# Seven block products in place of eight for two projections of an mLSTM and attention layer

## The chip, the cores and the metric

The kernel runs on one core of one Trainium2 chip. The metric is the device time of one execution in microseconds (us); a kernel's time is the median of its runs. The engines are called PE (TensorE, the matrix products), DVE (VectorE), ACT (ScalarE), POOL (GpSimd) and SP (SyncE, whose queue issues the weight loads). Each runs its own instructions strictly in the order in which they stand, apart from PE's weight loads, and semaphores tie the engines together.

## The reference

One layer on 512 tokens of width 1024, with 16 learned meta tokens ahead of them. The input is normalised, `h = rms_norm(x)`, and one large product `z = h @ w_in` is cut into the inputs of two branches: a forgetting attention with 8 heads ("FoX") and an mLSTM with 4 heads. Cut to what matters here:

```python
z = h @ w_in
(fq, fk, fv, ff, fz, mqk, mv, mi, mf, mo, mz, ga, gb) = jnp.split(z, SPLIT_POINTS, axis=-1)
...
hb = mlstm_scan(mq, mk, mv, log_ib, log_fb)                 # 4 heads, value width 512 each
hb = jax.nn.sigmoid(mo).reshape(B, L, 4, 512) * hb          # the gate "mo", 2048 columns of w_in
hb = rms_norm(hb, g_head.reshape(4, 512)).reshape(B, L, 2048)
yb = (hb * jax.nn.silu(mz)) @ w_b                           # "mz", 2048 columns of w_in
merged = jax.nn.sigmoid(ga) * ya + jax.nn.sigmoid(gb) * yb
return x + rms_norm(merged @ w_o, g_post)
```

The two projections that the change touches are `mo` and `mz`: per head, 512 tokens by 1024 times 1024 by 512 each.

## The kernel before

**Products.** Every fp32 product is three products of a faster type: a matrix is split into a high part (ACT, Copy, L121) and a low part (DVE, matrix minus high part, L123), and `mm3` (L128 to L131) accumulates high by high, high by low and low by high in PSUM. `hh` and `hl` are the parts of the transposed, normalised input (8 slices of 128 rows, 528 tokens) and are made once. A weight chunk of 128 x 1024 fp32 is loaded by SP (`wload`, tag `raw`, 3 buffers), split by ACT and DVE (`wsplit`, tags `whi` and `wlo`, 4 buffers), and used by PE.

**PSUM.** `psum2` is a pool of two tiles of two banks, `psum1` one of four tiles of one bank. A product that wants a `psum2` tile waits until the readers of the tile two before are through.

**The mLSTM heads** (L626 to L651, four rounds): `decay(h)` (row `nm` from memory, POOL adds a mask to make `dm`, ACT makes 14 blocks of `w` by Exp), `turn_part(h-1)` (PE transposes `ht` to `pht`, times `gz`, split into `bh` and `bl`), `conv_part` for q and for k (products `pqk`, ACT to `z` and `y`, three DVE steps for the taps, sigmoid `sg`, split into `qkh`, `qkl`), `wb_part(h-1)` (products `pyb`), `v_part`, `score_part` (products `ps`, times `w`, split into `wh`, `wl`), `mo_part`, `value_part`, `mz_part`. A scheduler then fixes the order of each engine's instructions, and mixes neighbouring parts.

- `mo_part` (L534 to L541): 96 matmuls 128x512 into two `psum2` tiles `po`, tokens on the partitions, then a sigmoid of each tile (L540) to `so`.
- `value_part` (L558 to L593): for each of four token chunks c, 6(c+1)+2 matmuls (`pna`, `pnb` for c = 0 and 1 in `psum1` tiles, `pnc` for c = 2 and 3 in `psum2` tiles), `r` from the normaliser, `ht` = product times `r` times `so` (L583), the square sum (ACT, L587), its power on POOL (`mrs`, L590), and the scaling of `ht` (L591).
- `mz_part` (L543 to L556): for u = 0 and 1, 48 matmuls 128x512 into one `psum2` tile `pz`, channels on the partitions, a sigmoid (L551), and two DVE steps (L554) to `gz`.

After the heads come the FoX branch, the gates, `w_a`, `w_o` and the output norm, which the change touches only in where tiles lie.

## Time and profile before

| | |
|---|---|
| median of 3 runs | 978.28 us (978.22 to 979.26) |
| the profiled execution | 978.2 us, span 976.4 us from the first to the last instruction |
| mean granted PE clock | 0.993 |
| matmuls, all | 5211 |
| from one head's first transposes to the next head's | 131.3 us |
| PE waits, longest | 3.4 us at 13.67 us; 1.5 us at 61.9 us |

The profile lists instructions by line, engine, operation and tile, with the start and the length of each. The length of a matmul is modelled and overlaps the next one; what a matmul costs in a full stream is the step from one start to the next. What lies outside the span, 1.8 us, is taken as fixed.

### The profile page before, as it was taken

What the parts mean: (1) busy time and instruction counts of PE and PEld (TensorE: products, weight loads), DVE (VectorE), ACT (ScalarE), POOL (GpSimd) and SP (SyncE); (2) the same over time, 40 slices, a digit from 0 to 9 for tenths busy, and PEclk for the clock granted to TensorE, in tenths of its full rate; (3) what the DMA queues carried; (4) which work ended last, traced back from release to release, by engine and by line L of the source; (5) the groups of instructions that cost most, each with busy time, mean ns of one, the idle gap of its engine ahead of it and who ended that gap; (6) DMA issues with size and microseconds to landing.
All of it is one profiled execution on the core that took longest, in us unless ns stands there. A gap on an engine that the chain in (4) does not pass through costs nothing.

```text
span 976.4 us, 12876 instructions
## 1 busy us (share of the span) xinstructions
PE 960.7 (98%) x5211; PEld 821.2 (84%) x5211; DVE 478.2 (49%) x792; ACT 376.6 (39%) x575; POOL 100.7 (10%) x164
## 2 busy tenths in 40 slices
PE   7999999999999999999999999999999999999997
PEld 5998889888898888988888888898888888888887
DVE  4795457344385235662444454446235446333443
ACT  4547335144252253441322333336233355322231
POOL 2152101001000001010000010214111112100000
PEclk7999999999999999999999999999999999999999
DMA  6233122323213322233232332333232322522312
GB/s 202 87 93 104 56 87 87 109 65 97 65 65 109 86 80 65 73 107 87 65 93 87 115 114 66 93 115 115 78 102 86 93 66 65 194 87 87 108 44 87
DMA packets 68214, 89.96 MB, mean 92 GB/s; under 512 B 4917, under 2 KB 50069, under 8 KB 68154
## 3 DMA queue, kind: packets, MB, share of 16 engines
q1 hardware_dynamic: 66072, 89.06, 30.2%
q8 instruction: 41, 0.67, 0.3%
q10 hardware_dynamic: 2082, 0.07, 0.1%
q14 instruction: 19, 0.16, 0.0%
HBM read 86.95 MB, written 2.16 MB: 91 GB/s over the span
## 4 chain that ended last, share of the span: by engine, by line
PE 91%; DVE 3%; ACT 3%; DMA 1%; issue 1%; ACTq 0%; POOL 0%; DVEq 0%; POOLq 0%
PE pv L129 3%; PE pv L130 3%; PE pv L131 3%; PE po L130 3%; PE pz L131 3%; PE po L129 3%; PE pz L130 3%; PE pz L129 3%; PE po L131 3%; PE pyb L129 3%; PE pyb L130 3%; PE pyb L131 3%; PE pqk L129 3%; PE pqk L131 3%; PE pqk L130 3%; PE pfk L129 2%
## 5 line engine op out<-in xcount | busy, mean ns | idle before, releaser
L123 DVE TENSOR_TENSOR wo_l<-wo_r,wo_h 128x1024 fp32r<-128x1024 f32 x24 | 29.5, 1230 | 67.0 <-ACT wo_h L121 67.0
L121 ACT ACTIVATE wo_h<-wo_r 128x1024 fp32r<-128x1024 f32 x24 | 25.1, 1056 | 72.5 <-PE pvm L166 49.0
L129 PE MATMUL pyb<-bh,wb_h 128*128 128x512 f32 x128 | 50.8, 397 | 0.0
L131 PE MATMUL pyb<-bh,wb_l 128*128 128x512 f32 x128 | 50.7, 396 | 0.0
L130 PE MATMUL pyb<-bl,wb_h 128*128 128x512 f32 x128 | 50.7, 396 | 0.0
L130 PE MATMUL po<-wo_l,hh 128*128 128x512 f32 x128 | 50.6, 395 | 0.0
L130 PE MATMUL pz<-hl,wz_h 128*128 128x512 f32 x128 | 50.5, 395 | 0.0
L129 PE MATMUL po<-wo_h,hh 128*128 128x512 f32 x128 | 50.5, 395 | 0.0
L131 PE MATMUL pz<-hh,wz_l 128*128 128x512 f32 x128 | 50.5, 394 | 0.0
L129 PE MATMUL pz<-hh,wz_h 128*128 128x512 f32 x128 | 50.4, 394 | 0.0
L131 PE MATMUL po<-wo_h,hl 128*128 128x512 f32 x128 | 50.4, 394 | 0.0
L129 PE MATMUL pv<-wv_h,hh 128*128 128x512 f32 (+1 forms) x128 | 47.0, 367 | 1.5 <-ACT y L486 1.5
L130 PE MATMUL pv<-wv_l,hh 128*128 128x512 f32 (+1 forms) x128 | 46.9, 367 | 0.0
L131 PE MATMUL pv<-wv_h,hl 128*128 128x512 f32 (+1 forms) x128 | 46.7, 365 | 0.0
L736 POOL TENSOR_SCALAR pn<-lt,rsum 128x128 f32<-128x128 f32 x32 | 24.1, 753 | 206.3 <-DVE rsum L734 206.3
L123 DVE TENSOR_TENSOR wz_l<-wz_r,wz_h 128x1024 fp32r<-128x1024 f32 x16 | 19.6, 1223 | 47.4 <-ACT wz_h L121 47.4
L493 DVE SCALAR_TENSOR_TENSOR y<-z,gc,y 128x512 f32<-128x512 f32 (+1 forms) x48 | 36.1, 754 | 3.2 <-ACT y L486 2.4
L129 PE MATMUL pqk<-hh,wq_h 128*128 128x258 f32 x128 | 36.5, 285 | 0.0
L129 PE MATMUL pqk<-hh,wk_h 128*128 128x264 f32 x128 | 36.4, 284 | 0.0
L129 PE MATMUL pfk<-hh,wfk_h 128*128 128x264 f32 x128 | 36.4, 284 | 0.0
L131 PE MATMUL pqk<-hh,wk_l 128*128 128x264 f32 x128 | 36.3, 284 | 0.0
L130 PE MATMUL pqk<-hl,wk_h 128*128 128x264 f32 x128 | 36.3, 284 | 0.0
(374 smaller groups left out, 2830.9 us busy)
## 6 DMA issues: line engine op xcount, KB each, us to landing
wv_r<-in_w_in_dram SPq DMA_DIRECT2D x16, 512.0 KB, 3.7
wo_r<-in_w_in_dram SPq DMA_DIRECT2D x16, 512.0 KB, 3.8
wz_r<-in_w_in_dram SPq DMA_DIRECT2D x16, 512.0 KB, 3.6
wb_r<-in_w_b_dram SPq DMA_DIRECT2D x16, 512.0 KB, 3.6
ab<-d_na SPq DMA_DIRECT2D x8, 672.0 KB, 3.8
wq_r<-in_w_in_dram SPq DMA_DIRECT2D x8, 512.0 KB, 3.5
wk_r<-in_w_in_dram SPq DMA_DIRECT2D x8, 512.0 KB, 3.7
wfq_r<-in_w_in_dram SPq DMA_DIRECT2D x8, 512.0 KB, 4.7
```

The costliest lines, as they stand in the source:

```text
L121: pin(S.activation(hi, raw, AF.Copy))
L123: pin(V.tensor_tensor(lo, raw, f(hi), ALU.subtract))
L129: T.matmul(ps, ah, bh, start=start, stop=False)
L130: T.matmul(ps, ah, bl, start=False, stop=False)
L131: T.matmul(ps, al, bh, start=False, stop=stop)
L493: V.scalar_tensor_tensor(y[:, t0:L], z[:, m, t0 + j:L + j], gc[:, j * 16 + mi:j * 16 + mi + 1], y[:, t0:L], ALU.mult, ALU.add)
L736: G.tensor_scalar(pn[:, o:o + P].rearrange("p (g t) -> p g t", g=4), lt[:, 0:32].unsqueeze(1).to_broadcast([P, 4, 32]), rsum, None, ALU.mult)
```

## The change

**The products.** Both projections are cut into 2 x 2 blocks (1024 inner rows into two halves of 512, 512 tokens into two of 256, the weight columns into two) and computed with one level of Strassen's algorithm in Winograd's form. With weight blocks a and token blocks b, seven products stand in place of eight: X = a11 b11, Y = s3 t3, Z = s1 t1, W = a12 b21, then Y += a22 t4, X += s2 t2, Z += s4 b22, where s1 to s4 are sums of weight blocks and t1 to t4 sums of token blocks. Each product of `mo_part` is 24 matmuls 128x256 (168 for a head), each of `mz_part` 12 for each u (168 for a head); 96 matmuls 128x512 stood in either place.

**What goes with it.** `st_tokens` makes t1 to t4 once, in head 0 between `columns()` and `decay(0)`: 7 additions of 1024 elements a partition on DVE, 3 on POOL (`l3`), four splits on ACT and DVE. For every head, `st_wide` makes the weight sums of `mo` with two additions of 128x1024 on POOL and two on DVE, and splits seven blocks of 1024 where four were split; `st_narrow` makes those of `mz` for each u with two additions of 128x512 on POOL and two on DVE, and splits one of 512 and three of 1024 where two of 1024 were split. Later products add to the same PSUM tiles, so ACT copies four partial results out of PSUM into `so` or `gz` on the way (`snap`), and three DVE steps combine them in PSUM (`st_decode`) ahead of the sigmoids.

```diff
+    def st_tokens():
...
+        for eng, l, a, b in ((V, l1, (0, 0), (0, 1)), (G, l3, (0, 1), (1, 1))):
+            eng.tensor_tensor(l, f(blk(hh, *a)), f(blk(hh, *b)), ALU.subtract)
+            eng.tensor_tensor(l, l, f(blk(hl, *a)), ALU.add)
+            eng.tensor_tensor(l, l, f(blk(hl, *b)), ALU.subtract)
...
+        for i, l in ((1, l1), (3, l3), (4, l4), (2, l2)):
+            hi, lo = t[i]
+            S.activation(hi, l, AF.Copy)
+            V.tensor_tensor(lo, l, f(hi), ALU.subtract)
...
+    def st_narrow(c0, name):
+        (r0,), (r1,) = (wload(win, 512 * i, 4, c0, 256, f"{name}{i}")[0] for i in range(2))
...
+        o = {"a11": split(r0[:, :, a], f"{name}a", ("whs", "wls"), mw, 1)}
+        G.tensor_tensor(r0[:, :, a], r0[:, :, a], r0[:, :, b], ALU.add)
+        G.tensor_tensor(r0[:, :, b], r0[:, :, b], r1[:, :, b], ALU.add)
+        x, y = split(r0, f"{name}b")
...
+        x, y = split(r1, f"{name}c")
...
+        V.tensor_tensor(r1[:, :, b], r0[:, :, a], r1[:, :, b], ALU.add)
+        V.tensor_tensor(r1[:, :, a], r1[:, :, a], r1[:, :, b], ALU.add)
+        x, y = split(r1, f"{name}d")
...
+        prod("X", "a11", "b11", False)
+        prod("Y", "s3", "t3", False)
+        S.activation(snap[:, 0], acc["Y"], AF.Copy)
+        S.activation(snap[:, 1], acc["X"], AF.Copy)
+        prod("Z", "s1", "t1", False)
+        S.activation(snap[:, 3], acc["Z"], AF.Copy)
+        prod("W", "a12", "b21", True)
+        prod("Y", "a22", "t4", True)
+        prod("X", "s2", "t2", True)
+        S.activation(snap[:, 2], acc["X"], AF.Copy)
+        prod("Z", "s4", "b22", True)
+    def st_decode(acc, both, snap, sv):
...
+        V.tensor_tensor(acc["X"], snap[:, 0], acc["X"], ALU.subtract)
+        V.tensor_tensor(both[1], both[1], s23, ALU.subtract)
+        V.tensor_tensor(both[0], both[0], s12, ALU.add)
...
     def mo_part(h):
-        w = wchunk(win, 0, KC, C_MO + h * MV, MV, f"wo{h}")
...
-        proj_wide(pn, w)
+        acc = {"W": pn[0][:, :, 0:256], "Z": pn[0][:, :, 256:512], "Y": pn[1][:, :, 0:256], "X": pn[1][:, :, 256:512]}
+        st_products(st_wide(c0, f"wo{h}"), acc, snap, True)
...
     for h in range(MH):
-        if h:
-            w = decay(h)
         if pend is not None:
             bt = turn_part(*pend)
         q = conv_part(h, 0)
         k = conv_part(h, 1)
+        if h:
+            w = decay(h)
...
             columns()
+            st_tokens()
             w = decay(0)
```

**Memory.** To make room, tiles share tags. `raw` has 4 buffers in place of 3. `nm`, `dm`, the square sums' scratch and the `y` of `turn_part` share a tag with two buffers; `z`, `w` and `so` share one; `ht` lies in the tiles of q's parts and `gz` in those of k's. `decay(h)` stands behind `conv_part` k in place of ahead of `turn_part`, so the row `nm` is asked for later on SP's queue. The FoX branch takes its scratch from another pool, and the output gain is loaded in two halves.

**The order at three places.** A row has the line, the operation, output and inputs, and in brackets the engines (or transfers, DMAHW) whose semaphores it waits for. The first place is head 1, from the end of `mo` into `value_part`. On ACT, before (`wz` are the weights of `mz`, split ahead for the next part; `so` is the gate):

```order
L121 ACTIVATE wz10_h1_2306<-wz10_r1_2300 128x1024 [waits DMAHW4_49,PE_49]
L121 ACTIVATE wz11_h0_2367<-wz11_r0_2363 128x1024 [waits DMAHW5_49,PE_49]
L540 ACT_TABLE_LOAD
L540 ACTIVATE so1_2042<-po1_0_2067 128x1024 [waits PE_49]
L540 ACTIVATE so1_2042<-po1_1_2068 128x1024 [waits PE_49]
L121 ACTIVATE wz11_h1_2371<-wz11_r1_2365 128x1024 [waits DMAHW6_49]
L587 ACTIVATE mjunk10_2184,mss10_2185<-ht10_2181 128x512 [waits DVE_49]
```

The table load waits for nothing and the two sigmoids for PE alone.

On ACT, now:

```order
L285 ACTIVATE so1_2268<-po1_0_2269 128x512
L222 ACTIVATE wz10b_h_2628<-wz100_r0_2618 128x1024 [waits PE_49,Pool_49]
L222 ACTIVATE wz10c_h_2632<-wz101_r0_2620 128x1024 [waits DMAHW3_49,PE_49,Activation_49]
L289 ACTIVATE so1_2268<-po1_1_2270 128x512 [waits PE_49]
L222 ACTIVATE wz10d_h_2638<-wz101_r0_2620 128x1024 [waits DVE_49,Activation_49]
L664 ACT_TABLE_LOAD [waits DVE_49]
L664 ACTIVATE so1_2268<-po1_0_2269 128x2x2x256 [waits Activation_49]
L664 ACTIVATE so1_2268<-po1_1_2270 128x2x2x256
```

Three splits (b, c, d) of the next part's weights stand among the copies, and the table load has a wait for DVE.

On DVE at the same place, now (`po1_1` and `po1_0` are combined by L297 to L299; `wz10d_l` is the low part of a weight sum of `mz`):

```order
L238 TENSOR_TENSOR wz101_r0_2620<-wz100_r0_2618,wz101_r0_2620 128x4x128 [waits DVE_49]
L239 TENSOR_TENSOR wz101_r0_2620<-wz101_r0_2620 128x4x128 [waits DVE_49]
L297 TENSOR_TENSOR po1_1_2270<-so1_2268,po1_1_2270 128x2x256 [waits Activation_49]
L298 TENSOR_TENSOR po1_1_2270<-po1_1_2270,so1_2268 128x1024 [waits DVE_49]
L224 TENSOR_TENSOR wz10d_l_2640<-wz101_r0_2620,wz10d_h_2638 128x1024 [waits Activation_49]
L299 TENSOR_TENSOR po1_0_2269<-po1_0_2269,so1_2268 128x1024 [waits PE_49]
```

These are the steps for which ACT's table load and sigmoids wait; the last one, L299, stands behind a split of the next part's weights. DVE had only such splits (L123) here before.

The second place is head 1, the second half of `mz` (`gz10` and `gz11` are u = 0 and 1; `wq2`, `wk2` are the next head's weights). On ACT, before:

```order
L587 ACTIVATE mjunk13_2290,mss13_2291<-ht13_2287 128x512 [waits DVE_49,Activation_49,Pool_49]
L121 ACTIVATE wq2_h0_2489<-wq2_r0_2485 128x1024 [waits DMAHW0_49,PE_49]
L121 ACTIVATE wq2_h1_2493<-wq2_r1_2487 128x1024 [waits DMAHW1_49,PE_49]
L551 ACTIVATE sz10_2359<-pz10_2310 128x1024 [waits PE_49]
L121 ACTIVATE wk2_h0_2625<-wk2_r0_2621 128x1024 [waits DMAHW2_49,PE_49]
L121 ACTIVATE wk2_h1_2629<-wk2_r1_2623 128x1024 [waits DMAHW3_49,PE_49]
L551 ACTIVATE sz11_2424<-pz11_2375 128x1024 [waits DVE_49,PE_49,Activation_49]
```

Nothing that PE needs in this part stands behind a sigmoid.

On ACT, now:

```order
L222 ACTIVATE wz11b_h_2748<-wz110_r0_2738 128x1024 [waits Pool_49]
L222 ACTIVATE wz11c_h_2752<-wz111_r0_2740 128x1024 [waits DMAHW5_49,PE_49]
L285 ACTIVATE gz10_2616<-pz10_2617 128x256 [waits PE_49]
L222 ACTIVATE wz11d_h_2758<-wz111_r0_2740 128x1024 [waits DVE_49,PE_49]
L289 ACTIVATE gz10_2616<-pz10_2617 128x256 [waits PE_49]
L121 ACTIVATE wq2_h0_2902<-wq2_r0_2898 128x1024 [waits DMAHW6_49,PE_49]
L282 ACTIVATE gz11_2736<-pz11_2737 128x256 [waits PE_49]
L283 ACTIVATE gz11_2736<-pz11_2737 128x256
L121 ACTIVATE wq2_h1_2906<-wq2_r1_2900 128x1024 [waits DMAHW7_49,PE_49,Activation_49]
L677 ACTIVATE gz10_2616<-pz10_2617 128x1024 [waits DVE_49,Activation_49]
L285 ACTIVATE gz11_2736<-pz11_2737 128x256 [waits PE_49]
```

The copies out of PSUM (L282 to L289) stand among splits for the next product and the next head, and the copy L285 of `gz11` stands behind a sigmoid that waits for DVE. The high part `wz11b_h` waits for POOL.

The third place is head 0, ahead of `score_part`. On POOL, before (`na` belongs to the attention's decay, `kr` to the meta tokens' keys):

```order
L429 COPY mr_500<-ac_477 12x4x16 [waits DVE_49]
L435 TENSOR_SCALAR na_506<-ac_477 8x528
L471 MEMSET z10_637 128x2x3 [waits DVE_49,Activation_49,Pool_49]
L510 CAST krh0_931<-qkh10_639 128x128 [waits Activation_49]
L510 CAST krl0_932<-qkl10_640 128x128 [waits DVE_49]
```

The meta tokens' keys follow the decay row and a clearing of `z10`.

On POOL, now (`yb` is `l3` of `st_tokens`; `wo000`, `wo001` are the weight sums of the first `mo`):

```order
L546 COPY mr_496<-ac_473 12x4x16 [waits DVE_49]
L552 TENSOR_SCALAR na_502<-ac_473 8x528
L588 MEMSET z10_633 128x2x3 [waits DVE_49,Activation_49,Pool_49]
L201 TENSOR_TENSOR yb_79<-hh_76 128x1024 [waits DVE_49,Pool_49]
L202 TENSOR_TENSOR yb_79<-yb_79,hl_77 128x1024 [waits Pool_49]
L203 TENSOR_TENSOR yb_79<-yb_79,hl_77 128x1024 [waits Pool_49]
L249 TENSOR_TENSOR wo000_r0_1013<-wo000_r0_1013,wo001_r0_1015 128x1024 [waits DMAHW6_49,DMAHW4_49,DMAHW7_49,DMAHW3_49,DVE_49]
L250 TENSOR_TENSOR wo001_r0_1015<-wo001_r0_1015,wo011_r0_1019 128x1024 [waits DMAHW5_49,DMAHW2_49,Pool_49]
L572 TENSOR_TENSOR dm0_936<-nm0_934,mask_t_384 128x512 [waits DMAHW4_49,DVE_49]
L627 CAST kr0_953<-qkh10_635 128x128 [waits PE_49]
```

Ahead of `kr`, POOL now has five additions of 128x1024 and the one of 128x512.

On ACT at the same place, now (`t3h` and `t1h` are high parts of token sums; `sg10` and `qkh10` belong to k):

```order
L602 ACTIVATE z10_633<-pqk101_689 128x528 [waits PE_49]
L603 ACTIVATE y101_738<-pqk101_689,gc_80 128x528 [waits DVE_49]
L210 ACTIVATE t3h_912<-yb_79 128x1024 [waits Pool_49]
L613 ACTIVATE sg100_744<-y100_686 128x528 [waits DVE_49]
L222 ACTIVATE wo0b_h_1027<-wo000_r0_1013 128x1024 [waits Pool_49]
L616 ACTIVATE qkh10_635<-y100_686 128x528 [waits DVE_49]
L613 ACTIVATE sg101_752<-y101_738 128x528 [waits DVE_49,Activation_49]
L210 ACTIVATE t1h_908<-yb_79 128x1024 [waits DVE_49]
L616 ACTIVATE qkh10_635<-y101_738 128x528 [waits DVE_49]
```

The sigmoid `sg100` of k stands behind `t3h`, which waits for POOL; before, it stood directly behind `y101`.

## The prediction

> **What bounds the kernel now.** I read the page's busy times and its chain first, then the stretch of one head, then the waits of PE. The page's busy times and its chain:

> ```profile
> PE 960.7 (98%) x5211; PEld 821.2 (84%) x5211; DVE 478.2 (49%) x792; ACT 376.6 (39%) x575; POOL 100.7 (10%) x164
> ...
> PE 91%; DVE 3%; ACT 3%; DMA 1%; issue 1%; ACTq 0%; POOL 0%; DVEq 0%; POOLq 0%
> ```

> One head's period (stretch, its length, then the busy time and count of PE, weight loads, DVE, ACT, POOL, the granted clock, DMA share, GB/s), and the two longest waits of PE:

> ```profile
> 134.60:265.90 131.30, 131.30 (x709) 112.67 (x707) 65.66 (x97) 50.70 (x77) 6.84 (x15) 1.00 0.28 83
> ```
> ```profile
> PE pv L129 <- POOL w0h_big_h L308: 3.4, 1, 3.4
> PE pv L129 <- ACT y L486: 1.5, 1, 1.5
> ```

> PE is the bound: in a head it never waits, at full clock, while DVE is half idle. So fewer PE cycles shorten the kernel one for one, as long as nobody makes PE wait; every new wait of PE lengthens it as directly. The forecast is a race between these two sums.

> **What PE saves.** What a matmul costs is the step from start to start. A stream of 128x512, first and last of 13, and one of 128x256, first and last of 20:

> ```profile
> 899.61 0.40 PE L131 MATMUL pya<-gh,wa_l 128*128 128x512 f32 x1
> ...
> 902.42 0.40 PE L131 MATMUL pya<-gh,wa_l 128*128 128x512 f32 x1
> ```
> ```profile
> 960.70 0.28 PE L131 MATMUL pout<-wo_h,ml 128*128 128x256 f32 x1
> ...
> 962.95 0.28 PE L129 MATMUL pout<-wo_h,mh 128*128 128x256 f32 x1
> ```

> That is 2.81/12 = 0.234 us and 2.25/19 = 0.1184 us: half the width costs 0.506 of the time, so Strassen loses almost nothing to narrow matmuls. Per head 192 x 0.234 = 45.0 us become 336 x 0.1184 = 39.8 us, 5.2 us less; four heads 20.8 us. It is the whole gain; what is added is on other engines.

> **What the others get.** The prices of the added work, from the groups: splits of 1024 (first DVE, then ACT), DVE steps that read PSUM (1024 and 512 elements), POOL steps, ACT copies out of PSUM (512, then 256 elements):

> ```profile
> L123 DVE TENSOR_TENSOR wo_l<-wo_r,wo_h 128x1024 fp32r<-128x1024 f32 x24 | 29.5, 1230 | 67.0 <-ACT wo_h L121 67.0
> L121 ACT ACTIVATE wo_h<-wo_r 128x1024 fp32r<-128x1024 f32 x24 | 25.1, 1056 | 72.5 <-PE pvm L166 49.0
> ```
> ```profile
> L624 DVE TENSOR_TENSOR yb<-pyb,yb 128x1024 f32<-128x1024 f32 x12 | 14.7, 1221 | 10.8 <-PE pyb L131 10.8
> L554 DVE SCALAR_TENSOR_TENSOR gz<-pz,gc,sz 128x512 f32<-128x512 f32 x16 | 11.2, 744 | 0.0
> L604 DVE TENSOR_TENSOR yt<-pht,gz 128x512 f32<-128x512 f32 x16 | 11.0, 690 | 1.7 <-DVE gz L554 0.5
> ```
> ```profile
> L707 POOL TENSOR_TENSOR yb<-yb,sgb 128x1024 f32<-128x1024 f32 x4 | 9.8, 2462 | 25.8 <-ACT sgb L706 25.8
> L590 POOL TENSOR_TENSOR mrs<-mss,mhalf 128x1 f32<-128x1 f32 x16 | 8.8, 551 | 185.4 <-DVE r L579 161.3 <-DVE mss L588 23.2 <-PE pnc L574 0.9
> ...
> L455 POOL TENSOR_TENSOR dm<-nm,mask_t 128x512 f32<-128x512 f32 x4 | 6.0, 1510 | 75.9 <-DMA nm<-d_nm 74.8 <-PE pcol L445 1.2
> ```
> ```profile
> L246 ACT ACTIVATE hh<-tr 128x512 fp32r<-128x512 f32 x8 | 4.8, 598 | 9.9 <-PE tr L244 9.7
> ```
> ```profile
> L862 ACT ACTIVATE ojunk<-pout 128x256 bf16<-128x256 f32 x8 | 3.1, 384 | 17.2 <-PE pout L131 17.2
> ```

> DVE per head: in `mo` five steps of 1.23 (three more low parts, two sums) and a decode of 0.69 + 1.22 + 1.22, together 9.3; in `mz` twice about 1.9 (low parts), 1.4 (sums), 1.8 (decode), about 10. ACT: 3 x 1.06 + 4 x 0.60 in `mo`, twice 0.63 + 1.06 + 4 x 0.38 in `mz`, about 12. POOL: 2 x 2.46 + 4 x 1.5, about 11. DVE goes from 65.7 to about 86 of a period near 126 us, so on average there is room. But all of it falls into the some 50 us from the start of `mo` to the end of `mz`, and much of it lies between two products of PE. So I followed PE's waits through that stretch by hand, with these durations and the new order of the queues (a start that follows another engine's end comes about 0.05 later); t is the time since the first matmul of head 1's `mo`.

> **Wait 1, into `value_part`.** Today ACT loads its table for the sigmoid while PE still multiplies, and the two sigmoids follow the two PSUM tiles; PE passes from `mo` to `value_part` without a gap:

> ```profile
> 231.09 1.28 ACT L540 ACT_TABLE_LOAD   x1
> 232.80 1.03 ACT L540 ACTIVATE so<-po 128x1024 f32<-128x1024 f32 x1 [0.42 <-PE po L131]
> 235.59 1.03 ACT L540 ACTIVATE so<-po 128x1024 f32<-128x1024 f32 x1 [1.76 <-PE po L131]
> ```
> ```profile
> 235.16 0.39 PE L131 MATMUL po<-wo_h,hl 128*128 128x512 f32 x1
> 235.39 0.28 PE L572 MATMUL pnb<-vh,wh 128*128 128x258 f32 x1
> ```

> In the new order the seventh product ends at t = 20.1 (168 x 0.1184, and 0.25 lost for a copy that W waits for). The X product is ready 2.8 us earlier; its copy and the split `wz10d` on ACT, then two decode steps and `wz10d_l` on DVE run to 21.3; the last decode step L299 takes 1.22 (22.5), the table load, which now has the wait for L299, 1.28 (23.8), the sigmoid 1.03 (24.8). Chunks 0 and 1 of `value_part` need only `psum1` tiles and keep PE busy for 22 matmuls, to 22.7. Chunk 2 wants the `po` tile and so the sigmoid: PE waits 2.2 us. If `wz10d_l` came behind L299 it would be 1.0; if DVE is late, 3.4.

> [...] A row decides for the load alone: the next instruction follows 1.29 us after its start.

> ```profile
> 77.36 1.28 ACT L447 ACT_TABLE_LOAD   x1
> 78.65 0.21 ACT L447 ACTIVATE col<-pcol 128x48 f32<-128x48 f32 x1
> ```

> **Wait 2, `mz` u = 1, Y.** The product Y needs the weight sum s3. POOL makes it (L232, 1.5) only when `wz11a_l` is through on DVE, which stands behind the four `ht` of `value_part`: 34.1 on DVE, 35.6 on POOL, `mrs` 0.55, L233 1.5 to 37.8, ACT's high part `wz11b_h` 39.0, DVE's low part 40.3. PE has run everything else by 38.4 (168 + 68 + 48 matmuls and the first transposes, some 34, and 4.2 of waits so far): 1.9 us (0 to 4).

> **Wait 3, `mz` u = 1, W.** W may start once Z's first part is copied out. On ACT that copy (L285) stands behind `wq2_h1` and the sigmoid of `gz10`, which waits for DVE's decode behind `wq2_l0`. PE is ready at 51.0 (all but the last 48 of `mz`'s matmuls, 356, and 16 transposes at no more than the same step make 44, waits 7). On ACT `wq2_h1` and the sigmoid end at 52.7 and the copy, 0.38, at 53.1: 2.1 us (0 to 4).

> **Small ones.** Four copies that W or Z waits for, 0.25 to 0.35 each (end of matmul, ACT start, 0.38 or 0.60, restart), 1.1; `pz10` for the PSUM tile of chunk 2, 0.6; `pz11` for chunk 3, 0.8; `pqk021` for the tile of `gz11`, 0.4; `pqk120` for an ACT step that stands behind the shared `y` buffers, 0.65; two more, 0.5. Together 4.1. A steady head then waits 2.2 + 1.9 + 2.1 + 4.1 = 10.3 us, against 5.2 saved; the bounds are 5 (each of the three at its lower end, most small ones hidden) and 14.

> **Head 0.** The token sums fall where DVE is nearly full, and POOL is slow there (a stretch by engines; then POOL's rows and ACT's sigmoid and high part of k, second half):

> ```profile
> 60.00:80.00 20.00, 18.52 (x154) 17.84 (x153) 17.47 (x24) 13.92 (x23) 8.47 (x10) 1.00 0.39 111
> ```
> ```profile
> 61.89 1.70 POOL L435 TENSOR_SCALAR na<-ac 8x528 f32<-8x528 f32 x1
> 63.54 0.09 POOL L471 MEMSET z<- 128x6 f32 x1
> ```
> ```profile
> 72.19 0.65 ACT L496 ACTIVATE sg<-y 128x528 f32<-128x528 f32 x1 [1.55 <-DVE y L493]
> 73.62 0.65 ACT L499 ACTIVATE qkh<-y 128x528 fp32r<-128x528 f32 x1 [0.77 <-DVE y L497]
> ```

> `l3` takes POOL to 63.6 + 3 x 2.46 = 71.0; `t3h` ends at 72.1 on ACT, and only then come the sigmoids of k, whose last high part moves from 73.6 to about 79. DVE has eleven steps of 1.23 more, 13.5 us, in a stretch with 2.5 us idle. The scores start late and PE waits about 4.4 us for them, 1.8 for the rest of `w` and the second POOL sum, and 3.4 into chunk 2: 9.6; the `mz` of this head as in the others, 7.5. That makes 17 (8 to 25).

> **The parts at nothing.** `decay` behind `conv_part` k, `nm` later on SP: `wb_part` and `v_part` lie between and cover it (by my count the weights `wv` keep 3 us of slack; without it PE would wait as long as it is late). The FoX branch keeps its order; its tiles only lie elsewhere.

> **The sum**, against the profiled execution (978.2, 0.1 us off the median): 978.2 - 20.8 + 17 + 3 x 10.3 = 1005 us. Its own range by the bounds: 978.2 - 20.8 + 8 + 15 = 980 to 978.2 - 20.8 + 25 + 42 = 1024.

> **Rival A, covered (faster).** The engines keep ahead of PE: the scheduler's order looks bad on paper, but a step that I place behind another may be ready early, since DVE is two thirds busy. With 2 us of waits per head the time is 978.2 - 20.8 + 8 = 965, from 957 to 976. It decides at 5.2 us of waits per head on average. For it: in all four heads of before PE waits for nothing. Against it: waits 1 to 3 are chains of dependent steps, not a lack of throughput.

> **Rival B, POOL is held up (slower still).** The same small POOL steps take several times as long where DVE is saturated, and `dm` costs 2.16 beside a busy DVE and 1.29 beside an idle one:

> ```profile
> 54.74 3.54 POOL L429 COPY mr<-ac 12x64 f32<-12x64 f32 x1
> 58.25 2.72 POOL L435 TENSOR_SCALAR na<-ac 8x400 f32<-8x400 f32 x1
> ```
> ```profile
> 76.56 2.16 POOL L455 TENSOR_TENSOR dm<-nm,mask_t 128x512 f32<-128x512 f32 x1 [1.17 <-PE pcol L445]
> ```
> ```profile
> 227.21 1.29 POOL L455 TENSOR_TENSOR dm<-nm,mask_t 128x512 f32<-128x512 f32 x1 [58.44 <-DMA nm<-d_nm]
> ```

> At 2.16/1.29 = 1.7 times, `l3` ends 5 us later and the sums of each head 3.5 us later: 1005 + 5 + 14 = 1024, from 1015 to 1035. [...]

> **Rival C, the clock.** After the early waits the granted clock was halved:

> ```profile
> 8.00:17.00 9.00, 5.30 (x21) 4.65 (x22) 5.31 (x8) 4.33 (x7) 2.85 (x13) 0.50 1.09 329
> ```

> Half of 5.30 busy us was lost there, 2.6. Two such drops a head would add 21 us: 1026. Against it stands the wait of 1.5 us inside 60 to 80, with the clock at 1.00. [...]

> **How the numbers follow.** About 0.2%, 2 us, is what a measurement of this kernel tells from no change. Forecast 0.62, A 0.14, B 0.13, C 0.07, and 0.04 that gain and waits cancel. Faster is A, 0.14; same 0.04; slower the rest, 0.82. The range 976 to 1026 leaves out most of A and half of B.

> **What would show it.** Right: in the changed profile, matmuls of 128x256 at steps of 0.118; PE waiting 1 to 3 us in each head at `pnc` for the sigmoid L664, at `pz` for L224 parts of a weight sum and for the copy L285; head 0's `ps` 3 us or more late behind `sg` and `t3h`. Wrong: PE waits under 5 us per head, or one wait that I have not named (SP's loads, the `y` buffers) larger than these.

## The result and the profile after

The changed kernel takes 1016.01 us (median of four runs, 1014.19 to 1017.4) beside 978.77 us before (978.22 to 979.4): ratio 1.0379, with a 95% interval of 1.0358 to 1.04. The forecast was 1005, slower, with a range from 976 to 1026. The profiled execution took 1017.04 us, its span 1015.3.

The page's busy times and its chain, in the changed kernel:

```profile
PE 959.9 (95%) x5787; PEld 846.4 (83%) x5787; DVE 580.9 (57%) x907; ACT 427.7 (42%) x657; POOL 151.0 (15%) x191
...
PE 73%; DVE 11%; ACT 7%; issue 4%; POOL 2%; DMA 2%; ACTq 0%; DVEq 0%; POOLq 0%
```

DVE is busy for 57% of the time and ACT for 42%; neither is a bound. Yet only 73% of the chain are PE's, 91% before: the rest are places where PE stood still for a step of DVE or ACT. One head's stretch in the changed kernel, the last of the three steady ones, cut at the same step of its round and the next one's, behind the first transposes (stretch, length, busy time and count of PE, weight loads, DVE, ACT, POOL, granted clock, DMA share, GB/s):

```profile
428.20:564.80 136.60, 130.06 (x851) 118.45 (x852) 85.22 (x124) 61.89 (x95) 17.13 (x19) 0.99 0.27 80
```

136.6 us stand where 131.3 stood (139.3 and 137.0 in the two heads ahead of it), DVE at 85.2 (forecast 86). The waits of PE, called the listed waits below (in all, how often, the longest):

```profile
PE pnc L698 <- ACT so L664: 11.1, 4, 4.6
PE ps L129 <- ACT qkh L616: 7.6, 2, 4.9
PE pz L129 <- ACT gz L285: 7.3, 4, 1.8
...
PE ps L129 <- DVE vm L181: 2.6, 2, 1.5
...
PE pqk L129 <- DVE gz L680: 1.5, 3, 0.5
...
PE pz L129 <- ACT wz11b_h L222: 1.2, 1, 1.2
...
PE pz L131 <- DVE wz11b_l L224: 0.6, 1, 0.6
```

These are the tiles and lines that the forecast named: `pnc` for the sigmoid, `pz` for the copy L285 and for the two parts of the weight sum `b`, `ps` in head 0 for k. What it did not have is the clock. Four stretches of 3.4 us around one wait of head 2 (columns as above):

```profile
393.30:396.70 3.40, 3.40 (x31) 3.40 (x30) 3.37 (x4) 1.06 (x1) 0.00 (x0) 1.00 0.53 154
396.70:400.10 3.40, 1.26 (x11) 1.05 (x10) 1.60 (x8) 2.61 (x3) 0.00 (x0) 0.99 0.50 154
400.10:403.50 3.40, 3.40 (x18) 3.40 (x17) 2.19 (x7) 1.95 (x5) 0.58 (x2) 0.51 0.00 0
403.50:406.90 3.40, 3.40 (x31) 3.40 (x30) 1.88 (x7) 0.72 (x2) 0.53 (x1) 1.00 0.00 0
```

In the second row PE waits 2.14 us for the sigmoid. In the third it never waits, but at clock 0.51 it gets through 18 matmuls where the fourth gets through 31: about 1.5 us lost after the wait is over. The profile has eight such stretches of 3.41 us inside the heads (four of them around head 0's score steps), the kernel before has none there.

From the starts of all matmuls, step by step against the full-clock step of the same form, the profiled execution divides like this; the listed waits each cost some 0.16 us more than the page's idle time, since the page puts the end of the last matmul later than the next start would have been (a matmul of 128x256 is listed with 0.28 us, and in a full stream the next one starts 0.118 after it):

| term, us | forecast | profile after |
|---|---|---|
| PE's saving | -20.8 | -19.4 |
| waits of head 0, small ones too | 17 | 21.8 |
| waits of heads 1, 2, 3 | 3 x 10.3 = 31 | 12.3, 9.7, 9.2 = 31.2 |
| matmuls at half clock | 0 | 9.2 (4.7 in head 0, 1.5 in each other) |
| faster steps by other tile places | 0 | -3.7 |
| sum with 978.2 | 1005 | 1017.3 |

The first wait of `pv`, ahead of the heads, was 3.4 us in the profile of before and 4.5 here, but it lies between 3.0 and 5.2 in all the profiles of this study without regard to the edit; it is left out, and the sum is good to about that much.

### The profile page after: what moved, and what is told of

It reads as the page before. It is cut to its first block, busy times and chain, and to the rows that moved or that the text cites. A ratio compares the mean times of both kernels' runs of the same rounds, so it can differ in the third digit from the quotient of the medians.

```text
span 1015.3 us, 14305 instructions
## 1 busy us (share of the span) xinstructions
PE 959.9 (95%) x5787; PEld 846.4 (83%) x5787; DVE 580.9 (57%) x907; ACT 427.7 (42%) x657; POOL 151.0 (15%) x191
## 3 DMA queue, kind: packets, MB, share of 16 engines
HBM read 86.95 MB, written 2.16 MB: 88 GB/s over the span
## 4 chain that ended last, share of the span: by engine, by line
PE 73%; DVE 11%; ACT 7%; issue 4%; POOL 2%; DMA 2%; ACTq 0%; DVEq 0%; POOLq 0%
PE pyb L130 3%; PE pyb L129 3%; PE pyb L131 3%; PE pv L129 3%; PE pv L130 2%; PE pv L131 2%; PE pqk L129 2%; PE pz L129 2%; PE pz L131 2%; PE pqk L130 2%; PE pqk L131 2%; PE pz L130 2%; PE po L129 2%; PE po L130 2%; PE po L131 2%
## 5 line engine op out<-in xcount | busy, mean ns | idle before, releaser
L866 POOL TENSOR_SCALAR pn<-lt,rsum 128x128 f32<-128x128 f32 x32 | 23.2, 726 | 210.9 <-DVE rsum L864 202.9
L131 PE MATMUL pyb<-bh,wb_l 128*128 128x512 f32 x128 | 49.8, 389 | 0.0
L129 PE MATMUL pyb<-bh,wb_h 128*128 128x512 f32 x128 | 49.8, 389 | 0.0
L129 PE MATMUL pv<-wv_h,hh 128*128 128x512 f32 (+1 forms) x128 | 47.0, 367 | 1.6 <-ACT y L603 1.6
L131 PE MATMUL pv<-wv_h,hl 128*128 128x512 f32 (+1 forms) x128 | 46.7, 365 | 0.0
L610 DVE SCALAR_TENSOR_TENSOR y<-z,gc,y 128x512 f32<-128x512 f32 (+1 forms) x48 | 41.3, 887 | 2.3 <-ACT y L603 1.6
L129 PE MATMUL pqk<-hh,wq_h 128*128 128x258 f32 x128 | 36.4, 284 | 1.5 <-DVE gz L680 1.5
L129 PE MATMUL pqk<-hh,wk_h 128*128 128x264 f32 x128 | 36.7, 287 | 0.8 <-ACT y L603 0.8
L129 PE MATMUL pfk<-hh,wfk_h 128*128 128x264 f32 x128 | 36.4, 284 | 0.0
L131 PE MATMUL pfk<-hh,wfk_l 128*128 128x264 f32 x128 | 36.4, 284 | 0.0
L131 PE MATMUL pqk<-hh,wk_l 128*128 128x264 f32 x128 | 36.3, 284 | 0.0
L130 PE MATMUL pfk<-hl,wfk_h 128*128 128x264 f32 x128 | 36.3, 284 | 0.0
L131 PE MATMUL pqk<-hh,wq_l 128*128 128x258 f32 x128 | 36.1, 282 | 0.0
L130 PE MATMUL pqk<-hl,wq_h 128*128 128x258 f32 x128 | 36.1, 282 | 0.0
L130 PE MATMUL pout<-wo_l,mh 128*128 128x256 f32 (+1 forms) x96 | 30.7, 320 | 0.0
L129 PE MATMUL pout<-wo_h,mh 128*128 128x256 f32 (+1 forms) x96 | 30.6, 319 | 0.0
L131 PE MATMUL pout<-wo_h,ml 128*128 128x256 f32 (+1 forms) x96 | 30.6, 318 | 0.0
L129 PEld LDWEIGHTS pv<-wv_h,hh 128*128 128x128 f32 x128 | 24.0, 188 | 6.1 <-ACT y L603 1.8
L698 PE MATMUL pnc<-vh,wh 128*128 128x258 f32 (+1 forms) x56 | 18.3, 328 | 11.1 <-ACT so L664 11.1
(1024 smaller groups left out, 3346.7 us busy)
```

The source lines that it names most:

```text
L129: T.matmul(ps, ah, bh, start=start, stop=False, **kw)
L130: T.matmul(ps, ah, bl, start=False, stop=False, **kw)
L131: T.matmul(ps, al, bh, start=False, stop=stop, **kw)
L610: V.scalar_tensor_tensor(y[:, t0:L], z[:, m, t0 + j:L + j], gc[:, j * 16 + mi:j * 16 + mi + 1], y[:, t0:L], ALU.mult, ALU.add)
L698: T.matmul(pn[u][:, 0:n], wh[:, s0:s0 + P], vh[:, j, o:o + n], start=(j == 0), stop=False)
L866: G.tensor_scalar(pn[:, o:o + P].rearrange("p (g t) -> p g t", g=4), lt[:, 0:32].unsqueeze(1).to_broadcast([P, 4, 32]), rsum, None, ALU.mult)
```

## Experiments

The first theory (**waits and clock**): the seven products save what they save in PE, the waits of PE for ACT and DVE cost their listed length, and those long enough cost half-clock stretches besides. Rivals: the products themselves save less than their count says; the clock does nothing (**waits alone**), and the loss lies in the memory layout or in contention. The diffs are against the changed kernel where nothing else is said.

**One projection at a time, and memory alone.** `mo` alone keeps the old `mz`:

```diff
+            w = wchunk(win, 0, KC, C_MZ + h * MV + u * 256, 256, f"wz{h}{u}")
...
-            st_products(st_narrow(C_MZ + h * MV + u * 256, f"wz{h}{u}"), acc, snap, False)
...
+            for m in range(2):
+                proj_t(ps[:, m, :], w, m)
```

> Strassen for the mo projection alone, with the new places of tiles; the mz projection has its eight products back. Theory (PE's work falls as forecast, and the waits that the changed profile shows are the whole loss): half of the saving, -10.4 us; head 0's waits for the scores (4.9 + 0.5 + 2.6 + 1.5 = 9.6 in the changed profile) and the four waits of chunk 2 (4.6 + 3 x 2.1 = 11.1) stay, and with them most of the stretches at half clock, some 7 us; so about 996 us, 990 to 1001. The waits at pz go, and their 19 us or so with them. Rival (the places of tiles and the later decay, or the narrow matmuls themselves, cost the time): half of the loss, about 997 to 1000, but without a wait at chunk 2 or at ps that explains it.

997.15 us (996.55 to 997.52), ratio 1.0178 (1.0161 to 1.0195). The time lies in both expectations; the waits, which are there, decide for the theory. The `pnc` wait is there four times, 9.7 us in all, and 7.0 us go to half-clock steps.

`mz` alone keeps the old `mo`:

```diff
+        w = wchunk(win, 0, KC, C_MO + h * MV, MV, f"wo{h}")
...
-        st_products(st_wide(c0, f"wo{h}"), acc, snap, True)
...
+        proj_wide(pn, w)
...
+            S.activation(so[:, 2 * i:2 * i + 2, :], pn[i], AF.Sigmoid)
```

> Strassen for the mz projection alone, with the new places of tiles; the mo projection has its eight products back. Theory: -10.4 us of PE work; the waits at pz in each head (1.2 + 0.65 + 1.8, and 0.5 + 0.3 at pqk, about 4.4, 18 us in all with their tails of 0.1 to 0.2 each) stay, head 0's waits for the scores shrink to some 6 (the additions for mo's weights on POOL are gone), chunk 2 waits no more; clock some 4: about 997 us, 990 to 1002. Rival: as for the kernel with mo alone; then PE's listed waits do not add up to the loss.

1005.99 us (1005.88 to 1007.8), ratio 1.0275 (1.0259 to 1.029): 4 us beyond the expectation's range. Its profile has 29.5 us of listed waits (without the warm-up's), 5.8 at half clock and 7.4 in many small ones; the small ones, at the copies out of PSUM, were counted too low. `mz` is the dearer half: it saves as much as `mo` and costs 9 us more.

With both old projections and no token sums, the memory and the place of `decay` are what is left of the change:

```diff
-        st_products(st_wide(c0, f"wo{h}"), acc, snap, True)
+        proj_wide(pn, w)
...
-            st_products(st_narrow(C_MZ + h * MV + u * 256, f"wz{h}{u}"), acc, snap, False)
+            for m in range(2):
+                proj_t(ps[:, m, :], w, m)
...
-            st_tokens()
```

> Both projections with their eight products, no token sums: only the new places of tiles, the later decay, four raw buffers. Theory: as before the change, 978.8 us within 2 us. Rival (sharing of buffers costs): 985 us or more, with waits of PE behind decay's w, the shared y buffers or the loads.

975.04 us (974.99 to 975.22), ratio 0.9955 (0.994 to 0.9969): faster, which neither theory had. In the heads PE waits only where it did before (1.6 us at `pv`), so `decay` further back is indeed covered. Most of the gain is in the steps of one product. Head 1's `pyb`, first and last of 96 matmuls in the kernel before:

```profile
290.61 0.39 PE L129 MATMUL pyb<-bh,wb_h 128*128 128x512 f32 x1
...
312.86 0.39 PE L131 MATMUL pyb<-bh,wb_l 128*128 128x512 f32 x1
```

And with the new memory alone:

```profile
290.37 0.39 PE L129 MATMUL pyb<-bh,wb_h 128*128 128x512 f32 x1
...
311.93 0.40 PE L131 MATMUL pyb<-bh,wb_l 128*128 128x512 f32 x1
```

22.25/95 = 0.234 us a step became 21.56/95 = 0.227: with 384 such matmuls 2.8 us, and 0.9 more from `pya` (0.2342 to 0.2297). The 128x512 matmuls of `po`, `pz` and `pv` keep theirs, 0.2325. The numbers multiplied are the same; what was changed for them is where their operands lie. The step stays at 0.227 in every kernel here with the new memory, whatever its other engines do beside it, so the places are the likely cause. Which of the moved tiles does it was not tried.

**The products without their costs.** All seven products run, on plain blocks; the sums, their splits, the copies and the combining steps are out:

```diff
-        G.tensor_tensor(r0[:, :, a], r0[:, :, a], r0[:, :, b], ALU.add)
-        G.tensor_tensor(r0[:, :, b], r0[:, :, b], r1[:, :, b], ALU.add)
...
+        o["s4"], o["s2"] = o["a12"], o["a22"]
...
-        S.activation(snap[:, 0], acc["Y"], AF.Copy)
-        S.activation(snap[:, 1], acc["X"], AF.Copy)
...
-            st_decode(acc, both, snap, sv)
```

> The seven products of each group run on plain blocks: the token sums, the weight sums, the copies out of PSUM and the combining steps are left out, so the two gates are not the reference's; PE does the same 336 narrow matmuls a head, the other engines what they did before. Theory: PE's saving alone is real, 978.8 - 20.8 = 958 us, 956 to 962, without waits over 0.5 us in the heads. Rival (matmuls of 128x256 do not hold their step of 0.118 us in these shapes, or W, X, Y and Z in shared PSUM banks slow PE): 965 us or more.

959.76 us (959.02 to 960.51), ratio 0.9798 (0.9784 to 0.9813). The new waits inside its heads are one row, 2.9 us:

```profile
PE pz L129 <- DVE r L664: 2.9, 4, 0.7
```

Against the 975.04 with the new memory and old products this is 15.3 us less: 19.4 saved, some 3.5 given back at that row (2.9 listed, and 0.16 for each of four). So the products save what their count says, to within 0.6 us. The rival that they don't falls, and what lies between 959.8 and 1016.0 comes with the sums, splits, copies and combining steps: PE's waits for them, and the clock.

**The clock.** Eight matmuls that nobody reads fill the wait for the sigmoid, so that PE is busy and resumes at the same time:

```diff
+                if c == 0:
+                    for _ in range(8):
+                        T.matmul(pn[1], hh[:, 0, NM:NM + P], hh[:, 0, NM:L], start=True, stop=True)
```

> The changed kernel with eight more matmuls of 128x512 ahead of value_part in each head (into a PSUM tile that is begun anew right after), so that PE works through most of the wait for chunk 2 in place of standing still; nothing else moves, and the wait itself stays where it is (PE's idle time at chunk 2 falls by 8 x 0.23 = 1.9 us in each head, the wait's end does not move). Clock theory (a wait of about 2 us inside one window of 3.4 us halves the granted clock for the next window): the half-clock stretches that begin behind chunk 2 in heads 0, 2 and 3 of the changed profile go or become fewer, 1.6 us each, so 1011 to 1014 us against 1016. Rival (the clock does not hang on these waits, or halving costs nothing): 1016 within 1 us with the same stretches. Third: the added matmuls lie on the path, 1020 or more.

The time decides nothing: the median, 1019.13 us, lies in none of the expected ranges, with 1014.82 in the profiled execution and 1018.75, 1020.14 and 1019.51 in the others; why those were longer stays open. The profile does. The same place in head 2 as above:

```profile
393.30:396.70 3.40, 3.13 (x25) 2.84 (x23) 2.05 (x7) 2.34 (x3) 0.00 (x0) 1.00 0.50 154
396.70:400.10 3.40, 3.38 (x28) 3.38 (x29) 2.30 (x6) 2.22 (x5) 0.55 (x1) 1.00 0.00 0
400.10:403.50 3.40, 3.17 (x27) 2.99 (x26) 1.94 (x9) 0.72 (x2) 0.66 (x2) 1.00 0.00 0
```

With the wait filled, the stretch behind it runs at 1.00, where it ran at 0.51, and so it does in head 3. In head 0, where 3.3 us of the wait are left, the slow stretch stays. Half-clock steps cost 4.8 us in this profile, 9.2 in that of the change, but not all of the difference is the filling's: of the stretches at waits that were not filled, two went and one came. That PE's standing still causes the slow stretch rests on this pair, on a count over nine profiles and on a comparison inside the last run, both further down.

**Mending the waits one by one.** First wait 1: L299 goes ahead of `wz..d_l` on DVE, and a small early sigmoid has ACT load its table while PE still multiplies:

```diff
+            with tc.issue_after(after.ins):
+                V.tensor_tensor(lo, src, f(hi), ALU.subtract)
...
+        x, y = split(r1, f"{name}d", after=LAST.pop("dec", None))
...
+        tc.keep_in_program_order(S.activation(tiny, mhalf, AF.Sigmoid))
+        LAST["dec"] = st_decode(acc, both, snap, sv)
```

> The changed kernel with the last combining step of mo ahead of the split wz..d on DVE, and the sigmoid's table loaded by a small sigmoid right behind the last copy. Theory (chunk 2 waits for exactly these two): the wait at pnc falls from 2.14 us to under 0.4 in heads 1 to 3 and by 2 in head 0, 9 us in all, and some of the half-clock stretches go with it: 1001 to 1007 us. Rival (DVE is simply full there, and the wait moves to ht and pz): 1011 us or more, with pz's wait for ht grown by as much.

1011.01 us (1009.53 to 1011.65), ratio 1.032 (1.0305 to 1.0335): the rival's range, but not by its mechanism, for `pz` waits for `ht` 0.8 us in all, where it waited 0.5. The wait is gone from heads 1 to 3; only head 0 still has one:

```profile
PE pnc L706 <- ACT so L672: 3.2, 1, 3.2
```

Listed waits (without the warm-up's and the first of `pv`) fall from 42.3 to 35.1 us, but half-clock steps still cost 8.9. A wait of 1.8 at `pz` that had done nothing to the clock now does:

```profile
286.30:289.70 3.40, 1.57 (x13) 1.34 (x13) 2.09 (x3) 2.24 (x3) 0.00 (x0) 0.98 0.45 154
289.70:293.10 3.40, 3.40 (x18) 3.40 (x18) 1.54 (x4) 0.00 (x0) 0.00 (x0) 0.52 0.47 154
```

In the changed kernel a wait of 1.83 us at the same tile, at 289.3, left the clock at 1.00. So which waits cost clock depended here on where they fell, and a mended wait gave back its length and not surely the 1.5 us behind it.

Then wait 3: Z's copy of u = 1 goes ahead of the sigmoid of u = 0 and of the next part's second split on ACT:

```diff
-        S.activation(snap[:, 3], acc["Z"], AF.Copy)
+        yield S.activation(snap[:, 3], acc["Z"], AF.Copy)
...
+                with tc.issue_after(after.ins):
+                    S.activation(g, ps, AF.Sigmoid)
```

> The changed kernel with the copy of Z of u = 1 on ACT ahead of the sigmoid of u = 0 and of the next part's second split. Theory (W of u = 1 waits for ACT's order alone): the wait of 1.82 us at pz in each head goes, 8 us with its tails: 1006 to 1010 us. Rival (it only moves on, to the next head's pqk that wants the tile of u = 0, or to Z's second part): 1013 us or more, with pqk's wait grown by 1 to 2 us.

1010.86 us (1010.08 to 1011.73), ratio 1.0321 (1.0305 to 1.0336): between the two expectations. The row of `pz` for the copy is gone (7.3 us) and the waits of `pqk` have not grown; listed waits, counted as above, are down from 42.3 to 33.8, and half-clock steps are up from 9.2 to 11.4. Again the wait was the one named, and the clock took a part back.

**Head 0.** Here the seven products run in heads 1 to 3 only, and `st_tokens` is written behind head 0's `mz`:

```diff
-            st_tokens()
...
-        so = mo_part(h)
+        so = (mo_part if h else mo_plain)(h)
...
+        gz = (mz_part if h else mz_plain)(h)
+        if h == 0:
+            st_tokens()
```

> Strassen in heads 1 to 3 only; head 0 has its eight products, and the token sums are made behind its mz part. Theory (head 0's loss is the token sums' place in the queues of POOL, ACT and DVE, with the clock behind it): its waits go, 18.7 us listed and some 8 of half clock, against 4.8 us of saving given up: 990 to 998 us; heads 1 to 3 as in the changed kernel. Rival (head 0's delays only move to head 1, where the token sums must be ready): 1005 or more.

1003.05 us (1001.17 to 1004.27), ratio 1.0237 (1.022 to 1.0254): too slow by 5. The scheduler put the token sums where they had been, ahead of k's sigmoids, although they were written later and wanted later:

```profile
PE ps L129 <- ACT qkh L616: 3.1, 2, 2.4
```

So they were written ahead of head 0's `mo` and held behind its score steps by force (against the kernel above; `END` holds the last of these steps on ACT, POOL and DVE):

```diff
+            with tc.issue_after(END[0].ins), tc.issue_after(END[1].ins), tc.issue_after(END[2].ins):
+                st_tokens()
```

> As the kernel with Strassen in heads 1 to 3 only, but with the token sums held on DVE, ACT and POOL behind the last step of head 0's scores (in the earlier kernel the scheduler had put them ahead of the scores all the same, and the waits of 0.7 + 1.0 + 2.4 + 1.1 + 1.1 us at ps were still there). Theory (those waits are the token sums' place in the queues): PE waits for nothing in head 0, 6.4 us of waits, 0.8 of tails and some 3 of half clock less: 991 to 996 us against 1003. Rival (the token sums' work, not their place, is what costs; then it turns up as waits in head 0's value_part or mz): 1000 or more.

997.67 us (995.71 to 998.47), ratio 1.0183 (1.0168 to 1.0198): 5.4 less, 1.7 above the theory's range and below the rival's. Of head 0's new waits one is left:

```profile
PE ps L129 <- DVE w L645: 0.9, 1, 0.9
```

The place of the sums in the queues, not their work, made head 0's scores late. 7.3 us still go to five half-clock stretches in heads 1 to 3.

**All mended together.** The kernel with late token sums (so the seven products in three heads, 14.5 us saved), both mends above, and u = 1's first split in other buffers:

```diff
+        o = {"a11": split(r0[:, :, a], f"{name}a", *((("whs", "wls"), mw, 1) if u == 0 else (("big_h", "big_l"), wk, None)))}
```

> Strassen in heads 1 to 3, the token sums behind head 0's scores, and in each head the last combining step of mo ahead of the next split with the table loaded early, the first split of u = 1 in buffers of its own (so that POOL's sums for it start earlier), and Z's copy of u = 1 ahead of the sigmoid of u = 0. Theory (the three ordering waits, the tokens' place and the half clock behind them are the whole loss): 975.0 of the kernel with the new places of tiles alone, less 3 x 4.8, plus some 2.5 of small waits a head: 968 us, 964 to 973, faster than the kernel before and than that one. Rival (DVE and ACT are full there, and each wait mended comes back at the next place): 978 or more.

976.91 us (975.87 to 979.83), ratio 0.998 (0.997 to 0.9991). No half-clock stretch is left in the heads, and 39 us of the 1016.0 are gone; but 968 was expected, 964 to 973, and the rival had 978 or more. Waits are still there:

```profile
PE pz L135 <- DVE ht L767: 2.7, 4, 0.8
...
PE pz L135 <- ACT gz L296: 1.3, 3, 0.4
PE pz L135 <- ACT wz31b_h L231: 1.1, 1, 1.1
PE pz L135 <- ACT wz11b_h L231: 1.1, 1, 1.1
PE pz L135 <- ACT wz21b_h L231: 1.1, 1, 1.1
```

With the small ones they are 15.9 us in three heads, 5.3 each, against 4.84 saved. Wait 2 (`wz..b_h`) did not go with the other buffers. These also hold the scores' parts until `value_part` is through with them, which is probably why; no run tried a third place.

**The best of it.** Only `mo`, in heads 1 to 3, with late token sums and wait 1 mended (against the late token sums):

```diff
+        tc.keep_in_program_order(S.activation(tiny, mhalf, AF.Sigmoid))
+        LAST["dec"] = st_decode(acc, both, snap, sv)
...
+            load = wload(win, 0, KC, C_MZ + h * MV + u * 256, 256, f"wz{h}{u}")
+            if u and "dec" in LAST:
+                with tc.issue_after(LAST.pop("dec").ins):
+                    w = wsplit(load)
...
-        gz = (mz_part if h else mz_plain)(h)
+        gz = mz_plain(h)
```

Here the splits held back are those of the plain `mz`, u = 1, on ACT and DVE both.

> Strassen for mo alone and in heads 1 to 3 alone, token sums behind head 0's scores, the last combining step ahead of the second half's splits of mz, the table loaded early; mz has its eight products. Theory (what mo's seven products save is kept where no wait is left; in mz the chain of sums, copies and combining steps takes back what they save): 975.0 of the new places of tiles, less 3 x 2.4, plus some 1 of small waits a head and 1 in head 0: 971 us, 968 to 974, below the kernel with both parts mended (976.9), without any half-clock stretch in the heads. Rival (the combining steps hold up ht and with it mz's first tile by as much as mo saves): 975 or more.

974.14 us (971.98 to 975.77), ratio 0.9947 (0.9934 to 0.9961): faster than before and 0.1 above the theory's range, but within its spread no faster than the 975.04 of the new memory with the old products. Most of its saving goes to waits again, among them one of `pz` for `ht`, whose longest is in head 3, and to one half-clock stretch:

```profile
PE pz L129 <- DVE ht L750: 3.0, 2, 2.6
...
PE ps L129 <- DVE w L652: 1.1, 1, 1.1
```

The same without the mend of wait 1 was to price the clock, as a pair (against the kernel just above):

```diff
-        tc.keep_in_program_order(S.activation(tiny, mhalf, AF.Sigmoid))
-        LAST["dec"] = st_decode(acc, both, snap, sv)
+        st_decode(acc, both, snap, sv)
...
-            load = wload(win, 0, KC, C_MZ + h * MV + u * 256, 256, f"wz{h}{u}")
-            if u and "dec" in LAST:
-                with tc.issue_after(LAST.pop("dec").ins):
-                    w = wsplit(load)
...
+            w = wchunk(win, 0, KC, C_MZ + h * MV + u * 256, 256, f"wz{h}{u}")
```

> The same without the two edits at the end of mo (the combining step stands behind a split of mz again, the table load behind the combining step): three waits of 1.9 us come back at chunk 2. Clock theory (such a wait costs itself, and where it fills over half of one of the windows of 3.4 us also a window at half clock, 1.6 us): 3 x 2.0 plus one to three times 1.6 above the mended one, 7.5 to 11 us, and not the same in every execution. Rival (a wait costs itself alone): 6 us, the same in each execution.

980.73 us (979.29 to 982.12), ratio 1.0017 (1.0008 to 1.0026), 6.6 more, between the rival's 6 and the clock theory's 7.5:

```profile
PE pnc L724 <- ACT so L666: 5.6, 3, 1.9
```

Both profiles have one half-clock stretch, so the pair doesn't separate the clock's cost. Listed waits explain 4.4 of the 6.6 (5.6 more at `pnc`, 1.2 less at `pz`), their ends about 0.5; the rest stays open.

Inside the second profile, though, stands a clean comparison. Its three waits at `pnc` are equal, 1.88 us each. These rows are cut at the edges of the 3.41 us windows (columns as above): the window with the wait, or with the larger part of it, and the window behind, for heads 1, 2 and 3.

```profile
238.94:242.35 3.41, 2.31 (x19) 2.31 (x20) 2.28 (x9) 2.85 (x6) 0.00 (x0) 1.00 0.62 193
242.35:245.76 3.41, 3.41 (x29) 3.25 (x28) 2.13 (x9) 0.45 (x2) 1.10 (x2) 1.00 0.00 0
368.65:372.06 3.41, 1.53 (x13) 1.32 (x12) 2.73 (x10) 3.20 (x3) 0.00 (x0) 1.00 0.69 201
372.06:375.47 3.41, 3.41 (x19) 3.41 (x18) 1.82 (x8) 1.36 (x5) 1.10 (x2) 0.50 0.31 109
501.77:505.19 3.42, 1.87 (x15) 1.87 (x16) 2.60 (x8) 2.86 (x4) 1.55 (x4) 1.00 1.02 368
505.19:508.60 3.41, 3.41 (x31) 3.41 (x30) 0.83 (x4) 0.88 (x4) 2.75 (x7) 1.00 0.30 103
```

Head 2's wait falls whole into one window, and the next one runs at 0.50. The other two are cut by an edge, 1.10 and 1.55 us of them in one window, and the clock stays at 1.00.

## Why the prediction was right, and where its sizes were off

**The sign and the bound.** PE bounds the kernel and every new wait costs its length: right. The run of the products without their costs shows the saving alone (959.8), and the other experiments show it eaten by waits, wait by wait.

**The saving.** 19.4, not 20.8: the step of `pya`, 0.234, was taken for all 128x512, while `mo` and `mz` ran at their own. First and last of head 1's 96 matmuls of `po`, before:

```profile
213.06 0.40 PE L129 MATMUL po<-wo_h,hh 128*128 128x512 f32 x1
...
235.16 0.39 PE L131 MATMUL po<-wo_h,hl 128*128 128x512 f32 x1
```

22.10/95 = 0.2326. Per head 192 x 0.2325 less 336 x 0.1185 is 4.84, not 5.2: 6% of the saving by a row taken from the wrong tile. The whole saving is 2% of the time, so the right row was worth looking up.

**The three waits of a steady head.** Right in place and size. Wait 1 in head 1, behind the first matmul of its `mo` (PE, DVE and ACT, PE again):

```profile
236.71 0.28 PE L129 MATMUL po<-wo1a_h,hh 128*128 128x256 f32 x1
...
256.94 1.22 DVE L224 TENSOR_TENSOR wz10d_l<-wz_r,wz10d_h 128x1024 fp32r<-128x1024 f32 x1
258.07 1.23 DVE L299 TENSOR_TENSOR po<-po,so 128x1024 f32<-128x1024 f32 x1
259.37 1.28 ACT L664 ACT_TABLE_LOAD   x1 [3.06 <-DVE po L299]
260.67 1.94 ACT L664 ACTIVATE so<-po 128x1024 f32<-128x1024 f32 x2
261.74 0.39 PE L698 MATMUL pnc<-vh,wh 128*128 128x258 f32 x1 [2.14 <-ACT so L664]
```

From 236.71 counted, L299 ends at t = 22.6 (forecast 22.5) and PE goes on at 25.0 (24.8), after 2.14 us (2.2). The sigmoid starts 1.30 after the start of the table load, which takes 1.28. Wait 2 is 1.2 and 0.6, together 1.8 (1.9), wait 3 is 1.8 (2.1), and the heads 1 to 3 have 10.4 us on average (10.3).

**Head 0.** 21.8 and not 17. The chain is the forecast's:

```profile
68.65 2.73 POOL L203 TENSOR_TENSOR yb<-yb,hl 128x1024 f32<-128x1024 f32 x1
...
71.41 1.06 ACT L210 ACTIVATE t3h<-yb 128x1024 fp32r<-128x1024 f32 x1 [1.46 <-POOL yb L203]
...
80.51 0.64 ACT L616 ACTIVATE qkh<-y 128x528 fp32r<-128x528 f32 x1 [3.41 <-DVE y L614]
81.20 0.79 PE L129 MATMUL ps<-qkh,qkh 128*128 128x512 f32 x1 [4.94 <-ACT qkh L616]
```

`l3` ends at 71.4 (forecast 71.0), `t3h` at 72.5 (72.1), k's high part at 81.2 (79): the last step was held up by DVE's `y`, by 3.4 us. DVE's added 13.5 us had been set against its idle time only and not followed step by step, and its steps grew besides. Here are one of POOL's additions with the DVE step beside it, the first token sum on DVE (beside another such addition), and the same kind of DVE step in head 1, with POOL idle:

```profile
63.35 2.40 POOL L201 TENSOR_TENSOR yb<-hh 128x1024 f32<-128x1024 f32 x1
63.41 2.91 DVE L610 SCALAR_TENSOR_TENSOR y<-z,gc,y 128x528 f32<-128x528 f32 x1 [0.44 <-POOL z L588]
...
76.50 3.36 DVE L201 TENSOR_TENSOR yb<-hh 128x1024 f32<-128x1024 f32 x1
...
184.16 0.77 DVE L610 SCALAR_TENSOR_TENSOR y<-z,gc,y 128x528 f32<-128x528 f32 x1 [0.20 <-ACT y L603]
```

Beside each of POOL's five additions of 128x1024 one DVE step with two inputs in SBUF took some 2.1 us longer than its 0.7 to 1.2, 10.7 us in all ahead of `y`. The count follows POOL's additions through the runs: five such steps ahead of the scores here and with `mo` alone, three with `mz` alone and with the seven products in heads 1 to 3 (both leave POOL only `l3` there), none before, with the memory alone and with the products alone. The scores waited 9.6 us (6.2), chunk 2 4.6 (3.4).

**Rival C, the clock: the step that failed.** It was given 0.07 because a wait of 1.5 us had left the clock at 1.00, and that row was read as if it held for 2 us. Nine profiles of kernels with the seven products show the difference: a full-clock window of 3.41 us in which PE was idle for more than 1.9 us was followed by a half-clock window in 16 of 16 cases, under 1.3 us in none, and between them in some. The forecast's waits of about 2 us sat at the edge of a bound that its row, at 1.5, could not show. So rival C holds as a part of the forecast case, 9.2 us and not 21, since a wait cost clock here only where its idle time fell into one window. It is the main reason why the time is 1016 and not 1005. That 1016 still lies in the range is partly luck: the clock's 9.2 us and the tiles' -3.7 were both put at nothing, and their signs differ.

**Rival A** falls with the waits (its remark that PE waits for nothing in any head of before passes over the 1.5 us at `pv` in head 0). **Rival B**, that DVE holds up POOL, falls with POOL's rows, one and the same addition in head 0 and in head 1:

```profile
73.16 2.85 POOL L249 TENSOR_TENSOR wo_r<-wo_r,wo_r 128x1024 f32<-128x1024 f32 x1 [1.78 <-DVE wo0a_l L224]
...
212.80 2.40 POOL L249 TENSOR_TENSOR wo_r<-wo_r,wo_r 128x1024 f32<-128x1024 f32 x1 [19.73 <-DVE wo1a_l L224]
```

In head 1 DVE does nothing meanwhile, so 2.40 is the undisturbed time. In head 0 DVE is busy all through it, and the addition takes 1.2 times as long; `l3` ends 0.4 us late, not 5. `dm`'s factor of 1.7 was no price for these additions. But where steps of the two ran side by side in head 0 they took longer, and DVE's paid more: two steps of L610 took 3.58 us from 73.00, where they take 1.57 from 184.16, beside POOL's 2.85 for 2.40.

**The parts at nothing.** `decay` behind k cost nothing (the run with the memory alone), but the tiles' new places were not nothing: 3.7 us in the kernel's favour. Without that and the clock, the forecast's own terms were off by 1.4 (the saving) and 5 (the waits, nearly all of it in head 0).

## What to carry to other kernels

Ask of a cheaper product not how much PE saves on average, but which chain of other engines' steps stands between two products, and follow each queue in order, with its steps as long as they are beside the other engines' steps of that place; for 19 us saved here 53 were paid in waits of 0.3 to 5 us, with DVE and ACT half idle. A wait of PE of about 2 us cost its length here, and in some heads some 1.5 us more in slow clock behind it, so a wait that the sum calls small should be set against the windows of 3.41 us measured here. When a change moves memory too, run the memory alone: here it was the only lasting gain, and the best version found (974.1 us) owes nothing measurable to the seven products.
